# Top-16 picks of the second sequence moved into the task queue, value sums tied behind the gate masks, and both expert tables stored block by block

## The chip, the cores and the metric

The kernel runs on one core of one Trainium2 chip. The metric is the device time of one execution in microseconds. TensorE (PE) multiplies matrices and has its own weight loads (PEld); VectorE (DVE), ScalarE (ACT) and GpSimd (POOL) do the rest. SyncE (SP) and POOL issue nearly all transfers, which share 16 DMA engines. All engines take their instructions in the order in which the program lists them, so an instruction that waits holds up everything listed behind it on that engine.

## The reference

Two sequences of 256 tokens (prompt and sample), model width 1024, go through the same layer: short gated convolution and attention side by side, an output projection, and then the part that fills most of the time, a PEER mixer with 16,384 experts:

```python
q = (xf @ wq).reshape(T, PEER_HEADS, 2, PEER_HALF)            # 8 heads, two halves
s = jnp.einsum('thpc,hpnc->thpn', q, subkeys)                 # 128 keys per half
sv, si = lax.top_k(s, PEER_TOPK)                              # 16 of 128
cand = sv[..., 0, :, None] + sv[..., 1, None, :]              # 256 pairs
cv, cp = lax.top_k(cand, PEER_TOPK)                           # 16 of them
gates = softmax(cv)
a = gelu(einsum('thkd,td->thk', u_tab[eidx], x)) * gates      # 128 experts per token
out = einsum('thk,thkd->td', a, v_tab[eidx])
```

Each expert has a row of 1024 floats in `u_tab` and one in `v_tab`, 64 MiB a table.

## The kernel before

**Two ways through the mixer.** The prompt's 256 tokens take the direct way: for each of 2 tiles of 128 tokens and each of the 128 picks, POOL gathers one row of u and v beside each other per token (`grow`, 128 x 2048 floats, 1 MiB, L178), 256 gathers in all. For each, DVE takes the dot product with x (L208, `grow<-grow,xh`), ACT makes gelu and gate of it (L197, `dots`), and DVE adds the weighted v row to the output (L188, `xh<-grow,dots,xh`, called the value sum below). Four buffers (a ring) hold gathered rows. The sample's 256 tokens take the dense way: all experts are computed on PE. 128 blocks of u, each 128 experts (`ub`, 512 KiB, L995), are multiplied with the normalised input (`pSj`, stage "experts"); a dense gate matrix is built beside this from one-hot masks (`oi`, `oj` on DVE, scaled to `gh`, `gl` on ACT, multiplied to `pgm` on PE, L919 and L920); gelu times gate lands in `Al` and `Ah`. Then 128 blocks of v are multiplied with these and summed in four PSUM banks (`acc`, L1046, stage "values", two blocks of 512 KiB a transfer, L1026). Every third value block is split into two parts of lower precision and takes three products.

**Order of the stages.** `front` (norm, convolution, attention, projection) of the prompt, its query projections and picks of tile 0, `front` of the sample beside the prompt's first gathers and the picks of tile 1, the sample's query projections (L885, `pqq`), experts, values.

**What sets the order around the change.** The prompt's gathers are interleaved with everything else by a credit rule. Each step of PE work calls `bg(us)` (L254): it adds `us * share["b"]` to a credit from which tasks (generators that yield their cost) are run, and `us * share["a"]` to a credit from which one `gather()` is made per 2.65 (`GU`); without tasks both shares go to gathers up to `SMAX`. A gather also waits for the PE instruction that was last listed when it was issued (`sync_dep`, L148). What is left of the 256 when the values begin (`left`, L1018) is spread evenly over the value blocks (L1049). The frame's scheduler then sorts the instructions of each engine; a manual dependency (`order`, L183) stops it from listing one ahead of another. In the kernel before, the sample's picks are not a task: `step1` (L860) lists them at once when a head's scores are there, with gathers mixed in by `SR`. Three half heads' scores stay behind (`lag=3`), and come after the first expert blocks (`rest`, L1002). `gates_dense` (L894) is the one task of the experts.

**Start.** `weights` (L112) loads a weight slice and at once lists its split into `whi` (ACT) and `wlo` (DVE); for the first slice that is before the norm of the first input tile (L494).

Of the kernel before, what the change touches and what calls it, by code (L numbers as in the profile page):

```python
# [8 lines left out]
F32 = mybir.dt.float32  # L9
# [3 lines left out]
AF = mybir.ActivationFunctionType  # L13
# [7 lines left out]
NC = 8  # L21
# [15 lines left out]
JH = 92  # L37
SR = 0.6
SS = 0.72
SMAX = 0.74  # L40
SPL = 3
SBS = 0.42


@with_exitstack
def encoder_layer(ctx: ExitStack, tc: tile.TileContext, xp, xs_, meta, vec, w_in, w_out, wq,
# [22 lines left out]
    dve = Recorded(nc.vector, last)  # L69
    act = Recorded(nc.scalar, last_act)  # L70

    def sb(name, bufs, side="left"):
        return tc.tile_pool(name=name, bufs=bufs, side=side, reuse_waits="tile")

    def ps(name, bufs):
        return tc.tile_pool(name=name, bufs=bufs, space=PSUM, reuse_waits="tile")
# [34 lines left out]

    def weights(src, s, split=False):  # L112

        w = [wtile("w").rearrange("p (c n) -> p c n", c=4) for _ in range(2)]
        for q in range(2):
            nc.sync.dma_start(w[q], src[:, s, 4 * q:4 * q + 4])
        if not split:
            return lambda c, k=0: w[c // 4][:, c % 4]
        k = 1 + 2 * spl[0]
        spl[0] = 1 - spl[0]  # L120
        hl = [ga[k + i].tile([P, 2 * D], F32R, tag="g", name=n).rearrange("p (q x) -> p q x", q=2)
              for i, n in enumerate(("whi", "wlo"))]
        for q in range(2):
            f = w[q].rearrange("p c n -> p (c n)")
            act.activation(hl[0][:, q], f, AF.Copy)
            dve.tensor_tensor(hl[1][:, q], f, hl[0][:, q].bitcast(F32), op=ALU.subtract)
        v = [x.rearrange("p q (c n) -> p (q c) n", c=4) for x in hl]
        return lambda c, k=0: v[k][:, c]

# [52 lines left out]

    def order(i, before):  # L183
        tc.add_manual_dep(i.ins, before.ins.name,
                          mybir.DependencyInfo(mybir.DependencyClass.NoSync, mybir.DependencyReason.DATA),
                          reason="order")

    def g_val():  # L188
        t, k, r = vals.pop(0)
        before = last[0]  # L190
        i = dve.scalar_tensor_tensor(gctx["h"], r[:, D:], dots[:, k:k + 1], gctx["h"], op0=ALU.mult, op1=ALU.add)
        order(i, before)
        if t == 0 and k == P - 1:
            pool.dma_start(yp[0:P, :], gctx["h"])
            gctx["h"] = gctx["next"][1]
# [18 lines left out]

    direct = [False]

    def gather(n=1):
# [43 lines left out]
    def more(us):  # L261
        credit["a"] += us
        while credit["a"] >= GU:
            credit["a"] -= GU
            gather()
# [109 lines left out]
    def projections(xr, sk, scores, qp, step=None, split=False, rescale=None, lag=1):  # L375

        rn = None
        late = []

        def key_scores(hp, qs, pl=None, tag="tr"):  # L380
            pn = (pl or pst).tile([P, 2, P], F32, tag=tag, name="pn")
            for t in range(2):
                pe.matmul(pn[:, t, :], qs[:, t * P:(t + 1) * P], sk[:, hp, :], start=True, stop=True)
            if hp < 2 and rn is not None:
                for t in range(2):
                    act.activation(scores[:, hp, t], pn[:, t], AF.Copy, scale=rn[:, t:t + 1])
            else:
                act.activation(scores[:, hp], pn, AF.Copy)
            if step is not None and hp % 2:
                step(hp // 2)  # L390

        for hd in range(PH):
            w = weights(wq, hd, split)
            for pp in range(2):
                pq = psm.tile([P, 256], F32, tag="mm", name="pqq")
                mm(pq, lambda c, k: w(c, k)[:, pp * P:(pp + 1) * P], xr, split=split)
                qs = qp.tile([P, 256], F32, tag="qs", name="qs", bufs=lag + 1)
                act.activation(qs, pq, AF.Copy)
                late.append((2 * hd + pp, qs))
                if len(late) > lag:  # L400
                    key_scores(*late.pop(0))
                if hd == 0 and rescale is not None:
                    rn = rescale(xr, pp)
                bg(3.9)
        if lag > 1:
            return lambda pl, tag: late and key_scores(*late.pop(0), pl, tag)
        key_scores(*late.pop(0))
# [20 lines left out]
    nc.sync.dma_start(vecs, vec)  # L428
    w_kv = weights(w_in, 0, True)
    nc.sync.dma_start(hs_[:, 1, :], xp[P:2 * P, :])  # L430
# [38 lines left out]
    def front(s, h, rn):  # L469
# [17 lines left out]
        for t in range(2):  # L487
# [5 lines left out]
            if sp:  # L493
                dve.tensor_scalar_mul(x, h[:, t, :], stat)  # L494
            else:
                act.activation(x, h[:, t, :], AF.Copy, scale=stat)
# [363 lines left out]
    def step1(hd):  # L860
        share["a"] = 0.0
        for us in heads1(hd, [0, 1]):
            more(us * SR)
        topk_left[0] -= 1

    rows = []

    def rescale(xr, pp):

        if pp == 0:  # L870
            on = q1.tile([P, P], F32, name="on", bufs=1)
# [11 lines left out]

    share.update(a=SR, b=0.0)
    rest = projections(xr1, sk1, sc1, q1, step1, rescale=rescale, lag=3)  # L885
    direct[0] = True
    pfs.close()
    psS = ctx.enter_context(ps("psS", 2))
    psgx = ExitStack()
    psg = psgx.enter_context(ps("psg", 2))  # L890
    r_done = [0]
    tau = [0]

    def gates_dense():  # L894
# [4 lines left out]
        topk_left[0] = -1  # L899
        yield 6.0  # L900
        ogx = ExitStack()
# [34 lines left out]
        for t in range(2):  # L936
# [14 lines left out]
            yield 1.6  # L951
            yield 3.0
            for o in range(P // OC):
                s0 = o * OC
# [5 lines left out]
                ib = iv[:, None, :, :].to_broadcast([P, OC, 64, 2])  # L960
                dve.tensor_tensor(v4(oi), sl4(0), ib, op=ALU.is_equal)
                dve.tensor_tensor(v4(oj), sl4(1), ib, op=ALU.is_equal)
# [4 lines left out]
                if len(steps) > 1:  # L967
                    gate_products(*steps.pop(0))
                if o == 0:
                    yield 2.0  # L970
                yield 1.3 + (4 * r_done[0] + 60) / 700
        gate_products(*steps.pop(0))
# [17 lines left out]
    for j in range(P):  # L990
# [3 lines left out]
        ub = wtile("u")  # L994
        nc.sync.dma_start(ub, u_t[:, j])  # L995
        if j % SG == 0:
# [6 lines left out]
        if j == 3:  # L1003
            tasks.append(gates_dense())
            share.update(a=SS, b=SBS)
        bg(3.5)
# [8 lines left out]
    acc = [[pacc.tile([P, 512], F32, name=f"acc{t}_{q}") for q in range(2)] for t in range(2)]  # L1015
    vn3 = v_n.rearrange("(i j) d -> i j d", j=P)
    vhl = gc.tile([P, 2, D], F32R, tag="xr", name="vhl")
# [4 lines left out]
    def values(j):  # L1022

        if j % 2 == 0:
            vpair[0] = vp.tile([P, 2, D], F32, tag="v", name="v")
            nc.sync.dma_start(vpair[0], vn3[:, j:j + 2])  # L1026
        vb = vpair[0][:, j % 2]
# [37 lines left out]
def layout(**inputs):  # L1065
# [15 lines left out]
    def wl(a):  # L1081
# [27 lines left out]
        qkg=qkg, gffn=g("norm_ffn_g"), rope=rope, iota16=iota, dec=dec,  # L1109
        u_t=c(u.reshape(P, P, NC, P).transpose(3, 1, 2, 0).reshape(P, P, D)), uv=c(np.concatenate([u, v], axis=1)), v_n=v)  # L1110

# [18 lines left out]
```

## Time and profile before

| | us |
|---|---|
| median of 3 runs | 1346.87 (1346.04 to 1347.17) |
| the profiled execution's own time | 1346.99 |
| its span, first to last instruction | 1345.2 |
| sample's query projections begin (first `pqq`) | 334.2 |
| experts begin (first `pSj`) | 408.6 |
| values begin (first `acc`) | 926.3 |
| last `acc` ends | 1341.1 |

1.8 us of the profiled execution lie outside its span. PE is busy in 95% of the span, DVE in 78%, and the DMA engines move 342 GB/s on average, over 410 GB/s in most slices of the second half. So no single engine is idle enough to be ruled out, and the question for each stage is which of PE and the transfers ends last. A busy PE is not one at its best: a matmul that runs at half clock counts as busy too, which is why the granted clock is read beside it.

### The profile page before, as it was taken

The numbers are of one execution on the slowest core, as the hardware profiler recorded it, in microseconds if no ns is written. First come the engines' busy times: TensorE is split into PE (matmuls) and PEld (weight loads), VectorE is DVE, ScalarE is ACT, GpSimd is POOL, SyncE is SP. The second block draws the span as 40 slices with busy tenths as digits, with TensorE's granted clock in tenths as the row PEclk, the third lists the DMA queues.
The fourth block names the chain that finished last, engine by engine and source line by source line (L and its number), as shares of the span: only waits on it lengthen the run. The fifth ranks groups of instructions, "written<-read, shape, count | busy, mean of one in ns | idle before, by whom it ended". The sixth has DMA issues, their size and how long they took to land.

```text
span 1345.2 us, 17868 instructions
## 1 busy us (share of the span) xinstructions
PE 1275.6 (95%) x6038; PEld 965.0 (72%) x6038; DVE 1056.0 (78%) x2279; ACT 549.9 (41%) x1621; POOL 389.1 (29%) x480
## 2 busy tenths in 40 slices
PE   6999998998898999969999999996999999999998
PEld 5888996777787887758888888884555555555554
DVE  5656998885799998679888787897677777777767
ACT  5555641742221311148776555663222222222221
POOL 1111223431223343543233232231222232222221
PEclk9999998998999999989999999997999999999999
DMA  5534636658998999999999999997999999999997
GB/s 174 160 108 152 214 106 219 216 192 317 365 333 309 383 417 415 416 412 386 399 396 399 397 415 354 409 403 275 410 420 422 421 420 415 420 420 418 415 422 324
DMA packets 80859, 459.68 MB, mean 342 GB/s; under 512 B 9456, under 2 KB 9968, under 8 KB 39552
## 3 DMA queue, kind: packets, MB, share of 16 engines
q0 software_dynamic: 37296, 270.02, 50.1%
q1 hardware_dynamic: 42032, 183.57, 35.9%
q10 hardware_dynamic: 1440, 4.95, 1.0%
q8 instruction: 47, 0.77, 0.2%
q14 instruction: 44, 0.36, 0.1%
HBM read 454.28 MB, written 4.19 MB: 341 GB/s over the span
## 4 chain that ended last, share of the span: by engine, by line
PE 37%; DMA 17%; DVE 7%; issue 3%; ACT 2%; POOL 0%; DVEq 0%; POOLq 0%; ACTq 0%; SPq 0%
PE acc L1046 27%; DMA grow<-in_uv,eidx 16%; PE pSj L136 9%; DVE xh L63 3%; DVE grow L63 2%; DMA v<-in_v_n 1%; DVE Ah L63 1%; ACT dots L63 1%; DVE Al L63 1%; PE pgm L920 1%; PE pgm L919 1%; ACT gh L63 0%; ACT pSj L63 0%; DVE vhl L63 0%; ACT gl L63 0%
## 5 line engine op out<-in xcount | busy, mean ns | idle before, releaser
L178 POOL DMA_INDIRECT grow<-in_uv,eidx x256 | 317.2, 1239 | 717.2 <-DVE xh L63 233.5
L136 PE MATMUL pSj<-xr,u 128*128 128x256 f32 x2048 | 468.9, 386 | 7.4 <-ACT Ah L63 4.7
L136 PEld LDWEIGHTS pSj<-xr,u 128*128 128x128 f32 x2048 | 386.2, 192 | 69.0 <-DMA u<-in_u_t 7.5
L63 DVE SCALAR_TENSOR_TENSOR xh<-grow,dots,xh 128x1024 f32<-128x1024 f32 x256 | 328.2, 1282 | 58.4 <-ACT dots L63 57.2
L63 DVE SCALAR_TENSOR_TENSOR grow<-grow,xh 128x1024 f32<-128x1024 f32 x256 | 312.5, 1221 | 70.2 <-DMA grow<-in_uv,eidx 69.2
L63 ACT ACTIVATE dots<-dots 128x1 f32<-128x1 f32 x256 | 51.7, 202 | 544.8 <-DVE grow L63 544.4
L1046 PE MATMUL acc<-v,Al 128*128 128x512 f32 x496 | 220.1, 597 | 5.1 <-DMA v<-in_v_n 5.1
L1046 PEld LDWEIGHTS acc<-v,Al 128*128 128x128 f32 x496 | 94.9, 191 | 113.0 <-issue 110.5
L1046 PE MATMUL acc<-vhl,ah 128*128 128x512 f32 x336 | 107.4, 441 | 0.0
L63 ACT ACTIVATE gh<-oj,ghi 128x128 f16<-128x128 f16 x256 | 99.5, 389 | 6.2 <-PE pgm L919 5.7
L63 ACT ACTIVATE gl<-oj,glo 128x128 f16<-128x128 f16 x256 | 99.5, 389 | 0.0
L63 DVE TENSOR_TENSOR vhl<-v,vhl 128x1024 fp32r<-128x1024 f32 x42 | 51.4, 1224 | 55.6 <-ACT vhl L63 55.6
L1046 PEld LDWEIGHTS acc<-vhl,ah 128*128 128x128 f32 x336 | 63.2, 188 | 30.2 <-issue 19.1
L1046 PE MATMUL acc<-v,Ah 128*128 128x512 f32 x192 | 84.3, 592 | 0.0
L63 ACT ACTIVATE dots<-dots,gate_all 128x1 f32<-128x1 f32 x256 | 74.6, 292 | 7.0
L63 DVE TENSOR_TENSOR wlo<-w,whi 128x1024 fp32r<-128x1024 f32 x42 | 51.1, 1218 | 19.6 <-ACT whi L63 13.4
L1046 PEld LDWEIGHTS acc<-v,Ah 128*128 128x128 f32 x192 | 36.4, 190 | 41.2 <-issue 40.2
L136 PE MATMUL pqq<-xr,w 128*128 128x256 f32 x256 | 60.0, 388 | 0.8 <-DMA w<-in_wq 0.8
L136 PEld LDWEIGHTS pqq<-xr,w 128*128 128x128 f32 x256 | 48.6, 195 | 8.1 <-DMA w<-in_wq 1.4
L919 PE MATMUL pgm<-gh,oi 128*128 128x128 f16 x256 | 36.8, 222 | 16.1 <-DVE oi L63 15.1
L63 ACT ACTIVATE vhl<-v 128x1024 fp32r<-128x1024 f32 x42 | 44.0, 1048 | 19.1 <-DMA v<-in_v_n 18.4
L63 ACT ACTIVATE whi<-w 128x1024 fp32r<-128x1024 f32 x42 | 43.9, 1058 | 18.3 <-PE pqq L136 8.5
(279 smaller groups left out, 1753.6 us busy)
## 6 DMA issues: line engine op xcount, KB each, us to landing
u<-in_u_t SPq DMA_DIRECT2D x128, 512.0 KB, 8.6
v<-in_v_n SPq DMA_DIRECT2D x64, 1024.0 KB, 8.9
w<-in_w_in SPq DMA_DIRECT2D x36, 512.0 KB, 3.9
w<-in_wq SPq DMA_DIRECT2D x32, 512.0 KB, 6.1
w<-in_w_out SPq DMA_DIRECT2D x16, 512.0 KB, 4.7
grow<-in_uv,eidx POOLq DMA_INDIRECT x256, 10.1
hdram<-h ACTq DMA_DIRECT2D x3, 512.0 KB, 2.7
h<-in_xp SPq DMA_DIRECT2D x2, 512.0 KB, 5.9
```

The source lines that it names most:

```text
L63: i = f(*a, **k)
L136: i = pe.matmul(out, st_(c, a), mv(c, b), start=(n == 0), stop=(n == NC * len(terms) - 1))
L178: i = pool.indirect_dma_start(out=r, out_offset=None, in_=uv, in_offset=bass.IndirectOffsetOnAxis(ap=eidx[:, t, k:k + 1], axis=0))
L919: pe.matmul(pg[:, q, :], oi[:, r, :], gh[:, r, :], start=True, stop=False)
L920: pe.matmul(pg[:, q, :], oi[:, r, :], gl[:, r, :], start=False, stop=True)
L1046: i = pe.matmul(acc[t][q], a[:, t * P:(t + 1) * P], v[:, q * 512:(q + 1) * 512], start=j == 0 and n == 0, stop=j == P - 1 and n == len(ter ...
```

## The change

There are five edits.

1. The sample's picks become tasks. `step1` only appends `heads1(...)` to the task list; the shares during the projections are a = 0.57 and b = 0.58 (was 0.6 and 0.0, with the picks listed at once), and they stay until the gate masks begin, where a = 0.75 and b = 0.46 (was 0.72 and 0.42 from block 3 on). `SMAX` is 0.66 (was 0.74). The gate task's yields are a little smaller.
2. A value sum may not be listed ahead of the newest `oi` mask on DVE.
3. `u_t` and `v_n` are stored so that one block is one contiguous run of memory; the load of block j is `u_t[j]`, of a value pair `v_n[j // 2]`. Bytes and shapes of the transfers are the same.
4. The split of the first weight slice is listed behind the norm of the first input tile.
5. The PSUM buffers of `pSj` are laid behind those of the gate products; and the row scale `rescale` of the sample comes two half heads later (4 scores instead of 2 are scaled on ACT).

```diff
-SR = 0.6
-SS = 0.72
-SMAX = 0.74
+SR = 0.57
+SRB = 0.58
+SSG = 0.75
+SMAX = 0.66
-SBS = 0.42
+SBS = 0.46
...
-    def weights(src, s, split=False):
+    def weights(src, s, split=False, late=False):
...
+        def convert(behind=None):
+            for q in range(2):
+                f = w[q].rearrange("p c n -> p (c n)")
+                act.activation(hl[0][:, q], f, AF.Copy)
+                i = dve.tensor_tensor(hl[1][:, q], f, hl[0][:, q].bitcast(F32), op=ALU.subtract)
+                if behind is not None:
+                    order(i, behind)
...
         order(i, before)
+        if last_oi[0] is not None:
+            order(i, last_oi[0])
...
-            if hp < 2 and rn is not None:
+            if hp < 4 and rn is not None:
...
-                if hd == 0 and rescale is not None:
-                    rn = rescale(xr, pp)
+                if hd < 2 and pp and rescale is not None:
+                    rn = rescale(xr, hd)
...
-                dve.tensor_scalar_mul(x, h[:, t, :], stat)
+                i = dve.tensor_scalar_mul(x, h[:, t, :], stat)
+                if t == 0:
+                    convert_kv(i)
...
     def step1(hd):
-        share["a"] = 0.0
-        for us in heads1(hd, [0, 1]):
-            more(us * SR)
-        topk_left[0] -= 1
+        tasks.append(heads1(hd, [0, 1]))
...
-    share.update(a=SR, b=0.0)
+    share.update(a=SR, b=SRB)
...
-    psS = ctx.enter_context(ps("psS", 2))
     psgx = ExitStack()
     psg = psgx.enter_context(ps("psg", 2))
+    psS = psgx.enter_context(ps("psS", 2))
...
-        yield 6.0
+        yield 3.0
...
+            share.update(a=SSG, b=SBS)
             for o in range(P // OC):
...
-                dve.tensor_tensor(v4(oi), sl4(0), ib, op=ALU.is_equal)
+                last_oi[0] = dve.tensor_tensor(v4(oi), sl4(0), ib, op=ALU.is_equal)
...
-                if o == 0:
-                    yield 2.0
-                yield 1.3 + (4 * r_done[0] + 60) / 700
+                yield 1.2 + (4 * r_done[0] + 60) / 760
...
-        nc.sync.dma_start(ub, u_t[:, j])
+        nc.sync.dma_start(ub, u_t[j])
...
-            share.update(a=SS, b=SBS)
...
-            nc.sync.dma_start(vpair[0], vn3[:, j:j + 2])
+            nc.sync.dma_start(vpair[0], v_n[j // 2])
...
-        u_t=c(u.reshape(P, P, NC, P).transpose(3, 1, 2, 0).reshape(P, P, D)), ..., v_n=v)
+        u_t=c(u.reshape(P, P, NC, P).transpose(1, 3, 2, 0).reshape(P, P, D)), ..., v_n=c(v.reshape(P, P // 2, 2, D).transpose(1, 0, 2, 3)))
```

The order shows three places. First, DVE at the start of the program, before (`ss` is the sum of squares, `xs` the normalised tile):

```order
L63 TENSOR_SCALAR ss_169<-ss_169 128x1
L63 TENSOR_TENSOR wlo<-w,whi 128x1024
L63 COPY sel<-ident 2x128
L63 TENSOR_TENSOR wlo<-w,whi 128x1024
L63 TENSOR_SCALAR xs<-h_123,stat 128x1024
```

And the same place after:

```order
L64 TENSOR_SCALAR ss_165<-ss_165 128x1
L64 COPY sel<-ident 2x128
L64 TENSOR_SCALAR xs<-h_123,stat 128x1024
L64 TENSOR_TENSOR wlo<-w,whi 128x1024 x2
L64 SCALAR_TENSOR_TENSOR lo<-pt,vecs,xT 128x128
```

Both `wlo` moved behind `xs`. Second, PE where the query projections (`pqq`, key scores `pn`) give way to the experts (`pSj`), before:

```order
L136 MATMUL pqq<-xr,w 128x256 x8
L383 MATMUL pn<-Ah,qs 128x128 x5
L136 MATMUL pSj<-xr,u 128x256 x16
L383 MATMUL pn<-Ah,qs 128x128
L136 MATMUL pSj<-xr,u 128x256 x8
L383 MATMUL pn<-Ah,qs 128x128 x2
L136 MATMUL pSj<-xr,u 128x256 x304
L938 LDWEIGHTS idx_i
```

And after, where the last row is again the first transpose of the gate stage:

```order
L149 MATMUL pqq<-xr,w 128x256 x8
L394 MATMUL pn<-Ah,qs 128x128 x2
L149 MATMUL pSj<-xr,u 128x256 x8
L394 MATMUL pn<-Ah,qs 128x128 x2
L149 MATMUL pSj<-xr,u 128x256 x8
L394 MATMUL pn<-Ah,qs 128x128 x2
L149 MATMUL pSj<-xr,u 128x256 x8
L394 MATMUL pn<-Ah,qs 128x128 x2
L149 MATMUL pSj<-xr,u 128x256 x376
L948 LDWEIGHTS idx_i
```

The late scores now stand one by one behind an expert block, and the gate stage begins after 400 `pSj` (50 blocks) instead of 328 (41 blocks). Third, DVE where the first masks are made, before:

```order
L63 TENSOR_TENSOR oj<-dup,io 128x512
L63 SCALAR_TENSOR_TENSOR xh<-grow,dots,xh 128x1024
L63 SCALAR_TENSOR_TENSOR grow,dots<-grow,xh 128x1024
L63 SCALAR_TENSOR_TENSOR xh<-grow,dots,xh 128x1024
L63 SCALAR_TENSOR_TENSOR grow,dots<-grow,xh 128x1024
L63 SCALAR_TENSOR_TENSOR xh<-grow,dots,xh 128x1024
L63 SCALAR_TENSOR_TENSOR grow,dots<-grow,xh 128x1024
L63 SCALAR_TENSOR_TENSOR xh<-grow,dots,xh 128x1024
L63 TENSOR_TENSOR oi<-dup,io 128x512
L63 SCALAR_TENSOR_TENSOR grow,dots<-grow,xh 128x1024
```

And after:

```order
L64 TENSOR_TENSOR oi<-dup,io 128x512
L64 TENSOR_TENSOR oj<-dup,io 128x512
L64 SCALAR_TENSOR_TENSOR xh<-grow,dots,xh 128x1024
L64 SCALAR_TENSOR_TENSOR grow,dots<-grow,xh 128x1024
L64 TENSOR_TENSOR oi<-dup,io 128x512
L64 TENSOR_TENSOR oj<-dup,io 128x512
L64 SCALAR_TENSOR_TENSOR xh<-grow,dots,xh 128x1024
L64 SCALAR_TENSOR_TENSOR grow,dots<-grow,xh 128x1024
L64 TENSOR_TENSOR oj<-dup,io 128x512 x2
L64 TENSOR_TENSOR oi<-dup,io 128x512
```

Before, four value sums and three dot products stood between the third `oj` group and the next `oi`; after, there is one pair between masks.

## Rows read from the trace of the kernel before

**Rows 1.** Busy time by stage: projections, experts (two parts), values; (x) counts instructions.

```profile
core 0: us, PE busy (x) PEld busy (x) DVE busy (x) ACT busy (x) POOL busy (x), PEclk, DMA share, GB/s
334.20:408.60 74.40, 65.38 (x322) 56.79 (x320) 63.28 (x263) 18.35 (x67) 20.82 (x44) 0.98 0.94 343
408.60:582.00 173.40, 171.22 (x761) 142.69 (x762) 150.28 (x365) 38.49 (x111) 72.09 (x71) 0.99 0.99 393
582.00:926.30 344.30, 321.07 (x1813) 277.26 (x1811) 286.29 (x445) 223.89 (x774) 106.09 (x87) 0.96 0.99 392
926.30:1341.10 414.80, 414.14 (x1192) 225.81 (x1192) 306.10 (x384) 103.55 (x281) 112.07 (x96) 0.99 0.98 406
```

**Rows 2.** PE's waits: for whom, us in total, times, longest us.

```profile
PE pgm L919 <- DVE oi L63: 15.1, 2, 9.6
...
PE acc L1046 <- DMA v<-in_v_n: 5.1, 1, 5.1
PE pSj L136 <- ACT Ah L63: 4.7, 1, 4.7
PE pb L877 <- ACT dg L63: 3.5, 1, 3.5
```

**Rows 3.** Busy time in three stretches at half clock (columns of Rows 1).

```profile
343.60:347.00 3.40, 3.40 (x10) 2.69 (x9) 2.44 (x7) 0.00 (x0) 1.00 (x1) 0.50 0.87 303
...
596.20:609.80 13.60, 7.03 (x22) 5.66 (x23) 11.40 (x18) 8.78 (x32) 5.75 (x5) 0.50 0.99 372
917.00:930.70 13.70, 5.47 (x14) 2.66 (x15) 5.81 (x10) 3.13 (x9) 1.18 (x1) 0.50 0.94 370
```

**Rows 4.** Expert blocks' own instructions in three stretches: PE, PEld, DVE, ACT, clock, DMA.

```profile
424.80:466.20 41.40, 41.40 (x194) 36.44 (x193) 0.00 (x0) 3.03 (x3) 1.00 0.96 365
510.50:555.90 45.40, 44.54 (x193) 35.54 (x193) 0.00 (x0) 3.01 (x3) 1.00 1.02 416
...
852.80:898.80 46.00, 43.45 (x193) 35.81 (x193) 3.09 (x3) 3.47 (x6) 1.00 1.02 409
```

**Rows 5.** Gate products' own instructions in the last of these: PE, DVE, ACT.

```profile
852.80:898.80 46.00, 5.52 (x75) 4.65 (x8) 1.11 (x5) 1.00 1.02 409
```

**Rows 6.** Value products' own instructions: PE, PEld, DVE, clock, DMA share, GB/s.

```profile
1005.50:1044.00 38.50, 38.50 (x114) 21.19 (x113) 0.00 (x0) 1.00 1.02 422
```

**Rows 7.** Instructions on gathered rows by stage: DVE, POOL (one per gather issued).

```profile
0.00:334.20 334.20, 41.94 (x52) 21.04 (x19) 0.98 0.54 185
334.20:408.60 74.40, 32.52 (x41) 13.85 (x14) 0.98 0.94 343
...
926.30:1345.20 418.90, 243.65 (x298) 112.07 (x96) 0.99 0.98 404
```

**Rows 8.** Timeline of the start: DVE and ACT; start, duration, [idle before <-releaser].

```profile
9.28 1.23 DVE L63 TENSOR_TENSOR wlo<-w,whi 128x1024 fp32r<-128x1024 f32 x1 [3.51 <-ACT whi L63]
...
10.94 1.06 ACT L63 ACTIVATE sq<-h 128x1024 f32<-128x1024 f32 x1 [0.27 <-DMA h<-in_xp]
...
11.85 0.75 DVE L63 TENSOR_SCALAR xs<-h,stat 128x1024 f32<-128x1024 f32 x1
...
13.80 0.37 ACT L63 ACTIVATE xT<-pt,vecs 128x128 fp32r<-128x128 f32 x1 [0.54 <-PE pt L461]
```

**Rows 9.** Timeline where the gate products begin: DVE and PE.

```profile
601.55 0.42 DVE L63 TENSOR_TENSOR oi<-dup,io 128x512 f16<-128x512 f16 x1
...
602.03 0.29 PE L919 MATMUL pgm<-gh,oi 128*128 128x128 f16 x1 [9.58 <-DVE oi L63]
```

**Rows 10.** SP's first value loads, and a stretch in which they alone run.

```profile
921.27 33.90 SPq L1026 DMA_DIRECT2D v<-in_v_n  x7
...
925.00:929.00 4.00, 2.74 (x4) 1.22 (x5) 0.00 (x0) 0.37 (x1) 0.00 (x0) 0.50 1.01 426
```

**Rows 11.** DVE groups during the projections: count, busy us, mean ns, idle before.

```profile
L63 DVE SCALAR_TENSOR_TENSOR xh<-grow,dots,xh 128x1024 f32<-128x1024 f32 x15 | 19.2, 1281 | 1.6 <-ACT dots L63 1.5
L63 DVE SCALAR_TENSOR_TENSOR grow<-grow,xh 128x1024 f32<-128x1024 f32 x13 | 15.7, 1209 | 8.1 <-DMA grow<-in_uv,eidx 8.1
```

More of the change, by code (lines that the diff above doesn't have):

```diff
@@ L70, in encoder_layer, with order @@
     act = Recorded(nc.scalar, last_act)
+    def order(i, before):
+        tc.add_manual_dep(i.ins, before.ins.name,
+                          mybir.DependencyInfo(mybir.DependencyClass.NoSync, mybir.DependencyReason.DATA),
+                          reason="order")
     def sb(name, bufs, side="left"):
@@ L122, in weights @@
               for i, n in enumerate(("whi", "wlo"))]
[L123 to L126, printed above, removed]
+        def convert(behind=None):
[5 more added lines that the diff above has]
+                    order(i, behind)
         v = [x.rearrange("p q (c n) -> p (q c) n", c=4) for x in hl]
+        if late:
+            return convert, lambda c, k=0: v[k][:, c]
+        convert()
         return lambda c, k=0: v[k][:, c]
@@ L181, in g_issue @@
         pend.append((t, k, r))
[L183 to L186, printed above, removed]
     def g_val():
@@ L215, in encoder_layer @@
     direct = [False]
+    last_oi = [None]
     def gather(n=1):
@@ L428, in encoder_layer @@
     nc.sync.dma_start(vecs, vec)
-    w_kv = weights(w_in, 0, True)
+    convert_kv, w_kv = weights(w_in, 0, True, True)
     nc.sync.dma_start(hs_[:, 1, :], xp[P:2 * P, :])
@@ L860, in step1, with rescale @@
     def step1(hd):
-        share["a"] = 0.0
-        for us in heads1(hd, [0, 1]):
-            more(us * SR)
-        topk_left[0] -= 1
+        tasks.append(heads1(hd, [0, 1]))
     rows = []
-    def rescale(xr, pp):
-        if pp == 0:
+    def rescale(xr, hd):
+        if hd == 0:
             on = q1.tile([P, P], F32, name="on", bufs=1)
@@ L1015, in encoder_layer @@
     acc = [[pacc.tile([P, 512], F32, name=f"acc{t}_{q}") for q in range(2)] for t in range(2)]
-    vn3 = v_n.rearrange("(i j) d -> i j d", j=P)
     vhl = gc.tile([P, 2, D], F32R, tag="xr", name="vhl")
@@ L1109, in layout @@
         qkg=qkg, gffn=g("norm_ffn_g"), rope=rope, iota16=iota, dec=dec,
-        u_t=c(u.reshape(P, P, NC, P).transpose(3, 1, 2, 0).reshape(P, P, D)), uv=c(np.concatenate([u, v], axis=1)), v_n=v)
+        u_t=c(u.reshape(P, P, NC, P).transpose(1, 3, 2, 0).reshape(P, P, D)), uv=c(np.concatenate([u, v], axis=1)), v_n=c(v.reshape(P, P // 2, 2, D).transpose(1, 0, 2, 3)))
 def kernel(**inputs):
```

## The prediction

> **What bounds the kernel now.** I read the profile in this order: busy time by stage, PE's waits, the clock, then the pace of the blocks in each stage. By stage [rows 1] PE is busy nearly all the time and the DMA engines too: from 408.6 us on both stand at 93% or more. So a stage can be bound by either, and the pace of the blocks tells which. Twelve expert blocks took 41.4 us where the transfers moved 365 GB/s, and 45.4 us where they moved 416 GB/s [rows 4]. The first is PE's own pace (3.45 us a block, no gate products in between); in the second, PE was slowed by the transfers. Twelve value blocks took 38.5 us at 422 GB/s [rows 6]; PE was busy throughout and waited for values only at the stage's start [rows 2], so I read that as PE's pace too (3.21 us a block), with the transfers just below their limit. PE's waits are few but long [rows 2], and three of them are followed by half clock [rows 3]: 1.2 instead of 2.4 GHz for 3.4, 13.6 and 13.7 us.
>
> I count transfers in units of 1 MiB (1.0486 MB): a gather is one, a value pair one, an expert block a half. At 416 GB/s a unit takes 2.52 us, at 422 GB/s 2.485 us. Four expert blocks with four gathers are 6 units, 15.1 us, which is what rows 4 show (45.4 / 3); with three gathers they are 5 units, 12.6 us, less than PE's 13.8.
>
> **The change part by part.** The sum goes by the profiled execution, 1346.99 us, of which 1345.2 us are span; it lies 0.1 us above the median of the runs shown.
>
> *Start.* The first tile's `xs` stood behind two `wlo` of 1.23 us until 11.85 us, and ACT's first `xT` began at 13.80 us [rows 8]. Afterwards `xs` needs neither, and `xT` follows ACT's second Square, which ends at 12.00 us. That gives 1.8 us; the `wlo` then lie beside PE's transposes. Bounds: 0 (the split's second half is needed next) and 4.4 us (back to the first `wlo`'s start at 9.28 us). I take 1.8, the nearer row.
>
> *Projections (74.4 us).* PE waited 3.5 us for the row scale (`pb` for `dg`) and 4.7 us for `Ah` before the first expert block [rows 2]. `pb` now stands 5 matmuls later (16 instead of 11 `pqq` behind the last transposes), 5 x 3.45 / 8 = 2.2 us; a wait of 1.3 us stays, and I let the half clock behind it go, worth half of 3.4 us. The 4.7 us go because `pSj` no longer takes the PSUM banks that the late scores must leave. Gain 2.2 + 1.7 + 4.7 = 8.6 us; at worst 0, when ACT stands behind a late dot product as before. The picks are now spread over the first 35 or so expert blocks. That they fit: DVE was busy 63.28 + 150.28 = 213.6 us from 334.2 to 582.0 [rows 1]. The order has 5 dot products fewer ahead of the first mask (48, was 53), 5 x (1281 + 1209) ns = 12.5 us [rows 11], so 201 us of work. PE needs 74.4 - 8.6 = 65.8 us, and 50 x 3.45 us more, 238 us to where the gate stage begins now. DVE has 37 us to spare.
>
> *Experts (517.7 us).* PE's own time is 128 x 3.45 = 441.6 us and 512 gate products at (46.0 - 41.4) / 75 = 0.061 us [rows 4, 5], 31.4 us, so 473 us. 44.7 us are lost. I can name 32: (a) blocks 20 to 43 at the transfers' pace, 24 x (45.4 - 41.4) / 12 = 8.0 us. (b) The first gate products: PE waited 9.6 us for an `oi` that stood on DVE behind value sums and dot products, which in turn waited for gathers [rows 2, 9], and then ran at half clock; 7.03 us of busy time there [rows 3] is 3.5 us lost. Together 13.1 us. (c) The end: 5.5 us for the last `oi` (15.1 - 9.6) and 5.1 us for the first value block, which SP could only issue at 921.27 us, behind the last gate products [rows 2, 10], and I put 0.7 us to half clock there, 11.3 us in all. Afterwards (a) goes: the credit rule gives 0.57 x 3.5 / 2.65 = 0.75 gathers a block (was 0.72 x 3.5 / 2.65 = 0.95). From the masks on it gives 0.99, but then PE has 13.8 + 32 x 0.061 = 15.8 us for four blocks against 15.1 us of transfers. Of (b) I leave 4 us: the tie puts the masks ahead of the value sums and the transfers are no longer behind, but only 3 blocks lie between the transposes and the first product, before it was 6. (c) goes: the last gate product now stands behind block 123, so nothing is left at the end and the first value pair is loaded beside the last blocks. Gain 8.0 + 9.1 + 11.3 = 28.4 us; bounds 0 (all three waits come back elsewhere) and 44.7.
>
> *Values (414.8 us).* Here the bill comes. Counting gathers through the credit rule, 99 are left for the value stage before and 110 after. The trace agrees with the 99: 96 were issued in that stage [rows 7], 3 before it. So 107 are to be issued, with 63 value pairs and 1 more unit: 171 x 2.485 = 424.9 us, and I add 3 us because the first gather waits for block 1. Before it was 161 x 2.485 = 400 us, below PE's 128 x 38.5 / 12 = 410.7 us. The stage turns from PE's to the transfers': 428 us, 13.2 us more. The half clock that cost 2.2 us at its start [rows 3] goes and is covered by that. Bounds for a unit: 2.46 us (426 GB/s, in a stretch in which value loads ran alone [rows 10]) and 2.52 us, so 421 and 434 us.
>
> *Layout.* I cost it at nothing. Value loads alone, with their old row distance of 512 KiB, moved 426 GB/s [rows 10], and the mix in the experts 416 GB/s [rows 4]: no row shows strided blocks to be slow. Bounds: 0, and what takes the value stage back to PE's pace (below). The Trainium skill, "DMA: Bandwidth & Descriptors", section "Latency and other measured facts", has copies with a row pitch of 512 KiB at 207 GB/s, and full rate when tiles are contiguous. [...]
>
> Sum: 1346.99 - 1.8 - 8.6 - 28.4 + 13.2 = 1321.4 us.
>
> **Rivals.** *Gathers slip (slower).* If the dot products and value sums, now tied behind masks that wait for PE, fall behind in the experts, gathers are issued late, since a ring buffer comes free only with its value sum. Each one that slips into the value stage costs 2.485 us there. For: at 408.6 us only 19 + 14 = 33 had been issued [rows 7] where the rule had listed 37, and ACT will be tight: 223.89 us of it [rows 1] for 64 mask steps is 3.5 us a step, against 3.94 us of PE per block and step. Against: DVE has 37 us to spare until the masks. From 10 late gathers on the gain is gone (25.6 / 2.485); with 12 late ones it is 1321.4 + 29.8 = 1351 us.
>
> *Waits in the mask stretch (less gain).* 31 blocks in a row now carry a mask step each. One event like the one at 602 us, 13.1 us, gives 1334 us. For: the ACT load. Against: with 25 products per four blocks PE lost nothing [rows 4, 5].
>
> *The gain is given back whole (no change).* The wait at the first gate products and those in the projections stay as they are, 9.1 + 8.6 us, and the values take 434 us, 6 us more: 1345 us. For: both hang on DVE's queue. Against: the transfers, for which that queue waited, have room now.
>
> *Layout counts (more gain).* If the contiguous blocks shorten every value load and leave gathers more room, the value stage falls back to PE's 410.7 us: 1304 us. Rows 10 speak against it; this is also the direction of the page's rule.
>
> **How the numbers follow.** Forecast 0.62, slipping gathers 0.14, waits in the mask stretch 0.12, given back whole 0.07, layout 0.05. A difference of 0.2% is what a measurement of this kernel can tell from none: 1344.2 to 1349.6 us. Faster is forecast, mask stretch and layout, 0.79; same 0.07; slower 0.14. The forecast's own range is 1310 (unit of 2.46 us, no wait left at the gates, 2.6 us more at the start) to 1336 us (unit of 2.52 us, 8.6 us of the projections not gained). The range that I give reaches from 1307 to 1345 us; outside are the slower case and most of the layout's.
>
> **What would show it.** Start: first `xT` near 12 us. Projections: first `pSj` 66 us or so behind the first `pqq`, with no wait for `Ah`. Experts: 13.8 us for four blocks up to block 48, no half clock of 13 us near the first `pgm`, none at the change to the values, first value load issued ahead of the last expert block; about 489 us in all. Values: longer than 414.8 us, about 428, with 107 gathers issued there, PE waiting for value loads or for ACT behind a dot product, and 420 GB/s or more. The forecast is wrong if the values stay near 411 us (then the transfers had more room than I think), if more than about 112 gathers are issued there, or if new waits stand between blocks 52 and 84.

## The result, and the profile after

The changed kernel takes 1359.16 us (1357.05 to 1361.19, four runs) against 1346.70 us before: ratio 1.0093 [1.0075, 1.0110]. It is slower by 0.9%, where 1321.4 us was forecast. The profiled execution took 1361.19 us, 1359.4 us of it span. (One of the twelve executions of e6 below took 4591 us; the median and the ratio shown there are those of the other eleven.)

By stage (projections, experts up to block 51, experts from block 52, values; columns of [rows 1]):

```profile
334.10:410.00 75.90, 66.90 (x316) 58.28 (x315) 52.49 (x184) 18.59 (x66) 23.24 (x37) 0.93 0.90 336
410.00:606.30 196.30, 187.28 (x849) 161.69 (x848) 157.98 (x439) 42.25 (x118) 64.33 (x76) 0.97 0.93 358
606.30:910.90 304.60, 297.55 (x1733) 259.05 (x1732) 260.65 (x412) 215.44 (x744) 90.53 (x78) 0.99 1.00 393
910.90:1354.40 443.50, 423.29 (x1193) 224.28 (x1191) 335.86 (x421) 108.92 (x306) 125.89 (x108) 0.99 1.00 411
```

The front ends where it ended before (334.1 us, 334.2). The projections take 75.9 us (forecast 65.8, before 74.4), the experts 196.3 + 304.6 = 500.9 (forecast 489.3, before 517.7), the values 443.5 (forecast 428, before 414.8). So 16.8 us were won in the experts and 28.7 us paid in the values. The columns on the right tell why: up to block 51 the DMA engines are busy 0.93 of the time and move 358 GB/s; before they were at 0.99 and 393 in nearly the same stretch [rows 1]. What was not moved there is moved in the values, where they are full (1.00). Gathers issued in the same four stretches (POOL's instructions that write `grow`):

```profile
334.10:410.00 75.90, 16.49 (x14) 0.93 0.90 336
410.00:606.30 196.30, 50.62 (x41) 0.97 0.93 358
606.30:910.90 304.60, 88.81 (x75) 0.99 1.00 393
910.90:1354.40 443.50, 125.89 (x108) 0.99 1.00 411
```

108 in the values stand against 96 before [rows 7]. PE's waits behind the front (for whom, us in total, times, longest):

```profile
PE acc L1053 <- DVE al L64: 18.3, 14, 2.7
PE pSj L149 <- ACT Al L64: 8.6, 2, 6.7
PE pgm L929 <- DVE oi L64: 6.3, 1, 6.3
PE pqq L149 <- DVE xr L64: 5.7, 1, 5.7
PE pt L750 <- DVE h L64: 3.3, 1, 3.3
```

The four waits of [rows 2] are gone or shorter, and others have come: for `xr` in the projections, for `Al` among the picks, for `oi` at the change from the first mask tile to the second (863.7 us), and fourteen for `al` in the values. With three of them goes half clock, as in [rows 3]:

```profile
359.60:366.40 6.80, 5.70 (x13) 4.55 (x14) 6.80 (x14) 0.45 (x3) 1.28 (x2) 0.50 0.93 348
489.30:496.10 6.80, 4.96 (x12) 3.98 (x13) 6.73 (x17) 2.66 (x6) 1.01 (x1) 0.50 0.78 320
861.40:868.20 6.80, 4.52 (x17) 3.82 (x18) 6.80 (x13) 5.16 (x20) 2.37 (x2) 0.50 0.93 338
```

The value products' own instructions in a stretch of 12 blocks, which took 38.5 us before [rows 6]:

```profile
1199.90:1243.40 43.50, 39.35 (x114) 20.94 (x113) 0.00 (x0) 1.00 1.01 418
```

At full clock and with the same 114 products PE now needs 43.5 us, with the DMA engines full: the transfers set the pace. The stage's full part and its end (columns of [rows 1]):

```profile
920.00:1340.00 420.00, 400.06 (x1130) 212.74 (x1129) 318.64 (x400) 103.21 (x292) 123.52 (x106) 0.99 1.01 416
1340.00:1354.40 14.40, 14.13 (x38) 6.74 (x36) 12.28 (x17) 3.24 (x10) 1.19 (x1) 1.00 0.64 258
```

While the DMA engines are full they move 416 GB/s, 2.52 us a unit of 1 MiB; in the last 14.4 us, when little is left to move, 258 GB/s.

### The profile page after: what moved, and what is told of

Same layout as the page of the kernel before. It is cut to its first block, busy times and chain, and to the rows that moved or that the text cites. A ratio compares the mean times of both kernels' runs of the same rounds, so it can differ in the third digit from the quotient of the medians.

```text
span 1359.4 us, 17884 instructions
## 1 busy us (share of the span) xinstructions
PE 1280.3 (94%) x6038; PEld 967.5 (71%) x6038; DVE 1054.7 (78%) x2276; ACT 550.6 (41%) x1622; POOL 384.9 (28%) x480
## 4 chain that ended last, share of the span: by engine, by line
PE 21%; DMA 18%; DVE 17%; issue 7%; ACT 5%; POOL 0%; DVEq 0%; POOLq 0%; ACTq 0%
DMA grow<-in_uv,eidx 18%; PE pSj L149 14%; DVE xh L64 7%; PE acc L1053 6%; DVE grow L64 4%; DVE Al L64 2%; ACT dots L64 2%; DVE vhl L64 2%; ACT vhl L64 1%; DMA v<-in_v_n 1%; ACT gh L64 1%; DVE al L64 0%; DVE Ah L64 0%; ACT Al L64 0%; ACT Ah L64 0%
## 5 line engine op out<-in xcount | busy, mean ns | idle before, releaser
L191 POOL DMA_INDIRECT grow<-in_uv,eidx x256 | 304.5, 1189 | 722.9 <-DVE xh L64 206.7
L1053 PE MATMUL acc<-vhl,al 128*128 128x512 f32 x168 | 49.0, 414 | 18.7 <-DVE al L64 18.3
L1053 PEld LDWEIGHTS acc<-vhl,al 128*128 128x128 f32 x168 | 29.8, 189 | 34.4 <-DVE al L64 29.2
L64 ACT ACTIVATE whi<-w 128x1024 fp32r<-128x1024 f32 x42 | 43.5, 1058 | 15.9 <-PE pqq L149 8.5
```

Source lines behind the costliest of these rows:

```text
L64: i = f(*a, **k)
L191: i = pool.indirect_dma_start(out=r, out_offset=None, in_=uv, in_offset=bass.IndirectOffsetOnAxis(ap=eidx[:, t, k:k + 1], axis=0))
L1053: i = pe.matmul(acc[t][q], a[:, t * P:(t + 1) * P], v[:, q * 512:(q + 1) * 512], start=j == 0 and n == 0, stop=j == P - 1 and n == len(ter ...
```

## The experiments

Theory A: the change is slow because its lower share of gathers in the projections and the first 50 expert blocks leaves 11 more for the values. Theory B: it is slow because of what it moved on DVE, ACT and POOL (picks, tie, masks). Each ratio is against the kernel before, run beside it, with its 95% interval; that kernel's own median there was 1343.9 to 1346.7 us, so rows are compared by their ratios; "left" counts the gathers that, in the order, still lack their dot product at the change to the values.

| kernel | left | values, us | median, us | ratio |
|---|---|---|---|---|
| before / changed | 99 / 110 | 414.8 / 443.5 | 1346.7 / 1359.2 | 1 / 1.0093 [1.0075, 1.0110] |
| e1 before, lower share | 110 | 446.1 | 1374.0 | 1.0225 [1.0199, 1.0250] |
| e2 changed, 11 left out | 99 | 413.5 | 1330.3 | 0.9899 [0.9874, 0.9924] |
| e3 before, new layout | 99 | 414.9 | 1345.1 | 0.9989 [0.9965, 1.0013] |
| e4b before, gate stage | 98 | 419.2 | 1338.8 | 0.9962 [0.9941, 0.9982] |
| e6 changed, share mended | 99 | 415.3 | 1338.9 | 0.9954 [0.9924, 0.9984] |
| e7 before, front parts | 99 | 415.3 | 1347.9 | 1.0022 [0.9993, 1.0051] |
| e9 e4b and e7 together | 98 | 419.8 | 1343.2 | 0.9986 [0.9962, 1.0010] |
| e10 before, tie alone | 99 | 413.4 | 1344.1 | 0.9980 [0.9952, 1.0007] |
| e11 e6, `cd` on DVE | 99 | 422.2 | 1346.8 | 1.0018 [0.9998, 1.0037] |
| e12 e6 without e7's parts | 99 | 415.5 | 1340.6 | 0.9979 [0.9953, 1.0004] |
| e13 e6, share moved | 99 | 418.9 | 1352.1 | 1.0044 [1.0019, 1.0068] |
| e14 e4b with a lull | 98 | 420.0 | 1341.2 | 0.9973 [0.9955, 0.9991] |

**e1, the lower share alone, on the kernel before.**

```diff
-SS = 0.72
+SS = 0.65
```

> The kernel before with one number changed: SS 0.65 instead of 0.72, so that 110 gathers are left for the value stage, as in the changed kernel (before 99). Nothing else of the change. Theory A (it is the share of gathers left for the value stage that costs): the transfers are idle more in the experts and the value stage grows by 11 units of 2.5 us, 27 us at most, while the experts win at most the 8 us of blocks 20 to 43; values 435 to 442 us, whole 1360 to 1368 us. Theory B (the ties and the picks as tasks make the value stage long, by dot products that stand in new places on DVE): values stay at 415 to 425 us and the whole at 1340 to 1350 us.

Experts (two parts) and values:

```profile
408.80:583.00 174.20, 172.33 (x770) 144.33 (x771) 151.66 (x368) 43.89 (x126) 71.99 (x71) 0.98 0.97 389
583.00:916.50 333.50, 317.61 (x1804) 274.89 (x1802) 259.07 (x409) 214.64 (x736) 88.16 (x76) 0.98 0.96 369
916.50:1362.60 446.10, 426.56 (x1192) 226.38 (x1192) 333.15 (x417) 107.53 (x303) 126.94 (x107) 0.98 0.98 403
```

One number makes the value stage as long as the whole change does, 31 us more; the experts win 10.0 us (507.7). B falls as the cause of the loss. A had the direction, and its sizes were too small: 446.1 us against 435 to 442 for the values, 1374.0 us against 1360 to 1368 for the whole. PE's waits near the first gate products in the same run:

```profile
PE pgm L919 <- ACT gh L63: 3.4, 1, 3.4
PE pSj L136 <- ACT Al L63: 0.3, 1, 0.3
```

The wait of 9.6 us for `oi` [rows 2, 9] is gone, without any tie; 3.4 us for `gh` stand there instead.

**e2, the changed kernel with 11 gathers of the second prompt tile left out** (their dot products and value sums too).

```diff
+    del queue[-11:]
     left = len(queue) + len(pend)
```

> The changed kernel, but 11 of the second prompt tile's 128 gathers (with their dot products and value sums) are left out, so that 99 stand before the value stage as before the change. Theory A (the units of transfer left over set the value stage): 443.5 - 11 x 2.52 = 416 us for the values, whole 1331 to 1334 us. Theory B (the waits of PE for al behind dot products, 18 us, set it): they do not go with the count, values 430 us or more, whole 1346 us or more.

```profile
905.20:1318.70 413.50, 412.67 (x1193) 224.46 (x1191) 308.78 (x388) 104.41 (x284) 116.69 (x97) 1.00 1.00 414
```

As A says: PE is busy for 412.67 of 413.5 us, and the waits for `al` are down from 18.3 to 0.2 us, so they were an effect of the 11 gathers. That it was their transfers, and not the work on DVE that went with them, is a reading: the DMA engines were full in both runs, DVE was busy for about three quarters of the stage in both. The 11 gathers cost 443.5 - 413.5 = 30 us, 2.7 us each. The row also shows that with 99 left the stage is at both limits: PE is full, and the DMA engines are at 1.00.

**e6, the changed kernel with the share mended; nothing is left out.**

```diff
-SR = 0.57
+SR = 0.70
```

> The changed kernel with one number changed: SR 0.70 instead of 0.57, so that 99 gathers are left for the value stage instead of 110; nothing is left out. Theory A (the share of gathers is what made the change slow, the rest of it is a gain): values back to 411 to 416 us, experts 505 to 512 us (11 more gathers there at 2.5 us, partly in transfer time that stood idle), whole 1334 to 1342 us, faster than before. Theory B (the picks as tasks and their waits eat the gain as well; with more gathers early the dot products stand behind transfers again): experts 515 us or more, whole 1345 us or more.

```profile
409.60:615.50 205.90, 188.94 (x850) 161.88 (x848) 179.54 (x496) 41.77 (x118) 84.15 (x92) 0.98 0.96 381
615.50:923.20 307.70, 300.73 (x1731) 259.25 (x1732) 264.18 (x421) 218.43 (x759) 95.48 (x80) 0.99 1.00 395
923.20:1338.50 415.30, 413.03 (x1193) 224.59 (x1192) 311.09 (x390) 104.95 (x286) 112.66 (x97) 1.00 1.00 414
```

A holds in the values and in the sign: faster than before, and 1.4% below the changed kernel (ratios 0.9954 and 1.0093). The experts take 205.9 + 307.7 = 513.6 us, between what the two theories gave: up to block 51, where 50 gathers were issued instead of 41, they take 9.6 us more than in the changed kernel (205.9 against 196.3), and behind it, with two gathers more, 3.1 us. PE's waits among the picks (first row) and in all of the mask stretch:

```profile
PE pSj L149 <- ACT Al L64: 14.7, 4, 5.3
PE pgm L929 <- ACT gh L64: 1.4, 1, 1.4
PE pgm L929 <- DVE oi L64: 1.0, 1, 1.0
```

So with the gathers back, the waits for `Al` grew from 8.6 to 14.7 us, but the long wait for `oi` at the first gate products did not return.

**e3, the layout alone.**

```diff
-nc.sync.dma_start(ub, u_t[:, j])
+nc.sync.dma_start(ub, u_t[j])
-nc.sync.dma_start(vpair[0], vn3[:, j:j + 2])
+nc.sync.dma_start(vpair[0], v_n[j // 2])
```

> The kernel before with the new layout alone: each expert block and each value pair one contiguous run in memory. My step cost it at nothing: 1346 to 1348 us, transfers in the value stage at 422 GB/s as before. The rival that layout counts: the value stage and blocks 20 to 43 shorter, 1338 us or less; or, if contiguous runs meet in the same banks, slower, 1350 us or more.

```profile
928.10:1343.00 414.90, 414.13 (x1192) 225.67 (x1192) 305.98 (x384) 103.40 (x281) 110.53 (x96) 0.99 0.98 406
```

No difference in time, and the values move 406 GB/s with either layout [rows 1]. There PE sets the pace, though (414.13 of 414.9 us busy), so the test of the layout is a stretch of expert blocks in which the transfers set it (columns of [rows 4]):

```profile
485.00:563.00 78.00, 76.72 (x336) 62.01 (x335) 0.00 (x0) 5.02 (x5) 1.00 1.02 416
```

That is the 416 GB/s of the old layout in that part of the experts [rows 4].

**e10, the tie alone** (the line in `g_val`, and `last_oi` set at each first mask).

```diff
+        if last_oi[0] is not None:
+            order(i, last_oi[0])
```

> The kernel before with the tie alone (a value sum never stands ahead of the last listed mask). My step (b) gave the tie most of 9.1 us at the first gate products: the wait for oi at 602 us (9.6 us) at most 4 us, half clock of 13.6 us gone, whole 1337 to 1341 us. Theory B (that wait comes from dot products that wait for gathers, which the tie does not move, and went in the changed kernel since the transfers were idle there): the wait stays above 7 us, whole 1344 to 1349 us.

```profile
PE pgm L922 <- DVE oi L63: 9.6, 1, 9.6
PE pgm L923 <- ACT gl L63: 0.8, 1, 0.8
```

The wait is the old one to a tenth, and so is the half clock behind it (13.7 us long). The time is not told apart from before. With e1: the wait came from dot products that stood ahead of `oi` and waited for gathers; fewer gathers took most of it away, the tie did not.

**e4b, the gate stage alone**: tie as in e10, and masks that end earlier.

```diff
-SBS = 0.42
+SBS = 0.44
-        yield 6.0
+        yield 3.0
-                if o == 0:
-                    yield 2.0
-                yield 1.3 + (4 * r_done[0] + 60) / 700
+                yield 1.2 + (4 * r_done[0] + 60) / 760
```

> The kernel before with the gate stage of the change alone: the value sums tied behind the masks, the masks listed earlier (3.0 instead of 6.0, 1.2 + (4 r + 60) / 760, SBS 0.44), but the picks of the second prompt as before, the share of gathers as before (98 left), old layout. Theory A (the loss is the share of gathers, while the mask step was priced rightly): the end of the experts wins the 11.3 us of my step (c), the value stage stays at 412 to 418 us; whole 1333 to 1339 us. Theory B (earlier masks push gathers out just as the whole change did): gathers issued in the value stage above 104, values 430 us, whole 1345 us or more.

Blocks 40 to 47, the rest of the experts, and the values:

```profile
551.10:599.90 48.80, 39.44 (x192) 31.69 (x193) 41.47 (x67) 32.48 (x114) 19.99 (x14) 0.90 1.00 398
599.90:913.20 313.30, 308.00 (x1736) 267.11 (x1733) 259.78 (x398) 198.88 (x685) 97.06 (x80) 0.99 0.99 394
913.20:1332.40 419.20, 414.03 (x1192) 225.97 (x1192) 309.63 (x388) 104.47 (x284) 110.46 (x97) 1.00 0.99 410
```

Theory A's side: faster, with 97 gathers in the values. The experts take 507.9 us, 9.8 us less than before. Of my step (c) the wait for `oi` is gone and 1.4 us for the first value block are left, but PE then waited 4.6 us for `vhl`, the split of the third value block, so the values are longer. And blocks 40 to 47 cost 48.8 us, where 64 gate products and 8 blocks need 31.5 (8 x 3.45 + 64 x 0.061).

**e7, three small parts alone**: late first conversion, row scale later (its diff below), PSUM order.

```diff
-if hd == 0 and rescale is not None:
-    rn = rescale(xr, pp)
+if hd < 2 and pp and rescale is not None:
+    rn = rescale(xr, hd)
```

> The kernel before with three small parts of the change alone: the late first conversion, the row scale later, and the PSUM order; read stage by stage. My forecast for them: start 1.8, row scale 3.9, wait for Ah 4.7, 10.4 us together, projections about 66 us long. Theory B, after the trace of the changed kernel: the start gives nothing (even again by 22 us), the 4.7 us go and come back as a wait for Al in the first 12 blocks, the row scale comes back as a wait behind a dot product; projections 72 us or more and the sum within 4 us.

Projections 74.8 us and ratio 1.0022: B. PE's waits in the projections and first blocks:

```profile
PE pqq L148 <- DVE xr L63: 3.1, 1, 3.1
PE pt L746 <- DVE h L63: 2.9, 1, 2.9
PE pb L886 <- ACT dg L63: 2.0, 1, 2.0
PE pn L390 <- ACT Ah L63: 1.8, 1, 1.8
```

The waits removed [rows 2] stand one step further on. The wait for `h` is not one of them: e3, e4b and e10, which are as before up to there, have it too (3.4 to 4.5 us).

**e9, e4b and e7's parts together**; of these the PSUM order:

```diff
-    psS = ctx.enter_context(ps("psS", 2))
     psgx = ExitStack()
     psg = psgx.enter_context(ps("psg", 2))
+    psS = psgx.enter_context(ps("psS", 2))
```

> All parts of the change but the picks as tasks, the share of gathers (98 left) and the layout: late conversion, row scale, PSUM order, tie, masks that end earlier. If the parts add, 1338.8 (the gate stage alone) less what the front parts give: 1330 to 1336 us, faster than both kernels. If the waits only move: 1338 us or more. Against the changed kernel with its share mended it tells what the picks as tasks are worth.

The parts don't add: not told apart from before, and no gain on e4b. Nor can it be told from e6, so what the picks as tasks are worth stays open.

**e12, e6 with the first conversion, row scale, PSUM order and layout as before.** What is left of the change, beside tie, masks and shares, is the picks as tasks:

```diff
-        share["a"] = 0.0
-        for us in heads1(hd, [0, 1]):
-            more(us * SR)
-        topk_left[0] -= 1
+        tasks.append(heads1(hd, [0, 1]))
```

> The back of the change alone with the mended share: picks as tasks, tie, masks that end earlier, 99 gathers left; first conversion, row scale, PSUM order and layout as before. Against the changed kernel with the mended share (1340.3) it tells what the front parts are worth there. My forecast gave them 10.4 us: then this one is at 1347 to 1351 us. Theory B (they are worth nothing or less, as the run of them alone says): 1334 to 1341 us.

Theory B: ratio 0.9979 beside e6's 0.9954, with intervals that overlap. The front parts are worth nothing that can be told in either company.

**e11, the pair sums of the picks on DVE, in e6.**

```diff
-pool.tensor_tensor(cd[:, :, o:o + n], s0[:, :, a:a + 1].to_broadcast([P, n_t, n]), ...
+dve.tensor_tensor(cd[:, :, o:o + n], s0[:, :, a:a + 1].to_broadcast([P, n_t, n]), ...
```

> The changed kernel with SR 0.70 (99 gathers left), and the pair sums of the picks (cd) on DVE instead of POOL. Theory A (the picks make PE wait for Al because POOL's queue couples them with the gathers: POOL stands at cd until DVE has come to the picks, 24 us in blocks 0 to 51, with the next gathers behind it): the waits for Al there, 14.7 us with the mended share, fall below 6 us, DVE grows by 10 us of small adds; whole 1328 to 1335 us. Theory B (DVE's own queue is full there and ACT's Gelu of Al stands behind weights of dot products): the waits stay at 10 us or more, whole 1338 to 1345 us.

PE's waits in blocks 0 to 51:

```profile
PE pSj L149 <- ACT Al L64: 11.6, 4, 5.8
```

14.7 us in e6: B. POOL's queue is not what makes the picks hold PE up. The whole, 1346.8 us, lies above B's range as well; the values took 422.2 us, and why was not found.

**e13, e6 with the gathers moved to the gate stage.**

```diff
-SR = 0.70
+SR = 0.64
-SSG = 0.75
+SSG = 0.80
```

> The changed kernel with 99 gathers left as in the run of the mended share, but the 11 moved elsewhere: SR 0.64 (was 0.57, mended 0.70) in the projections and the picks' blocks, SSG 0.80 (was 0.75) in the gate stage. Theory A (in the gate stage PE's own pace of 15.8 us for four blocks still covers 6.24 units, 15.7 us, while each gather among the picks makes waits): blocks 52 on stay at 15.8 us for four, experts some 506 us, whole 1333 to 1338 us. Theory B (only the number left counts, not where they go): 1338 to 1343 us, with blocks 52 on at 16 us or more for four.

Worse than either theory gave. From block 52 to the values PE waited four times for `oi`:

```profile
PE pgm L929 <- DVE oi L64: 7.6, 4, 2.5
```

Blocks 96 to 119 took 109.0 us (98.9 for blocks 96 to 119 in e6). Where the gathers go counts too. That the masks stand behind dot products on DVE there fits the four waits; no run isolates it.

**e14, e4b with a lull in the gathers ahead of the masks.**

```diff
+            share["a"] = 0.75
+        if j == 32:
+            share["a"] = 0.45
```

> The kernel before with the gate stage of the change (tie, masks that end earlier), and a lull in the gathers ahead of the first masks: the share of gathers is 0.45 instead of 0.72 from block 32 to the first mask, some 4 gathers fewer there, and 0.75 behind it, so that 98 are left for the value stage as without the lull. Theory A (the wait for oi and the half clock at the first gate products come from dot products that wait for late gathers, so transfers that have room there take it away; this, not the tie, is what the changed kernel won at that place): blocks 40 to 47 take some 31 us instead of 48.8, whole 1322 to 1332 us, faster than every kernel so far that computes everything. Theory B (DVE and ACT are full with masks there, whatever the transfers): blocks 40 to 47 stay at 44 us or more, whole 1337 us or more.

Not decided: the sizes are theory B's, but the edit did not do what it was meant to. 36 gathers were issued up to block 39, as many as in e4b, and 12 instead of 14 in the next eight blocks:

```profile
411.50:557.70 146.20, 53.13 (x36) 0.99 0.97 384
557.70:602.50 44.80, 16.80 (x12) 0.89 0.99 393
```

I read this as gathers that had been listed before block 32 and were late, so that the lull came too late for the place it was meant for. Blocks 40 to 47 took 44.8 us (48.8 in e4b), and the whole gained nothing on e4b.

e4b and e6 both beat the kernel before (by 0.4% and 0.5%) and the changed kernel.

## Why the prediction was wrong

The miss is 1361.19 - 1321.4 = 39.8 us of the profiled execution: values 15.5, experts 11.6, projections 10.1, start 1.7, end 0.9.

*Values (+13.2 forecast, +28.7).* The mechanism was right and the count nearly so (108 gathers issued, 107 forecast): the stage turned from PE's to the transfers'. The failed step is the term 171 x 2.485. Its rate came from one stretch of 422 GB/s, in which PE set the pace [rows 6]; the changed kernel moved 416 GB/s where the transfers set it, 2.52 us a unit, and 258 in its last 14.4 us, so 411 GB/s and 2.55 us a unit over the whole stage. 443.5 us at that rate are 174 units. 3 units x 2.485 + 174 x 0.066 - 3 us (the allowance at the start) are the 15.5 us, roughly. From the same step came a slack of 10.7 us between PE and the transfers before. e2 shows none: the 11 units cost 30 us, all of their time. (The lower bound of 421 us leaves out the 3 us that 428 and 434 include.) With this term right the forecast would have been 1336.9 us, still faster; with this miss alone taken away the changed kernel would be at 1345.7 us, as before. So it takes this miss and the others together to make the kernel slower, and e1 and e6 show that the value stage's part hangs on one number, the share.

*Experts (-28.4 forecast, -16.8).* (c) came true: block 124 to the values took 13.9 us (27.5 before), and no half clock stood there. (b) came true at its place and for another reason: the first gate product at 609.8 us waited for nothing, but e10 shows that the tie alone does nothing there and e1 that fewer gathers do. In the changed kernel fewer gathers are not the whole of it: e6 has as many left as before, and PE waits 1.4 us there. What else took the wait away (the picks spread out, the gate stage nine blocks later, the masks listed earlier) was not isolated; the tie and the masks listed earlier, without the rest, leave a wait of 5.5 us for `oi` (e4b). Of the 16.8 us won, 12.7 were bought with the gathers that the values paid for (500.9 against e6's 513.6). What failed is "DVE has 37 us to spare", from which I had the picks fit. Busy time fitted; order did not. ACT's Gelu of `Al` stood behind weights of dot products and an Exp that waited for DVE, PE waited 8.6 us, and half clock followed. The longer of the two waits ended at 491.14 us; on ACT (`gate_all` is the Exp's; start, duration, [idle before <-releaser]):

```profile
484.16 0.20 ACT L64 ACTIVATE dots<-dots 128x1 f32<-128x1 f32 x1 [3.85 <-DVE grow L64]
...
488.45 0.31 ACT L64 ACTIVATE gate_all<-gate_all 128x128 f32<-128x128 f32 x1 [2.45 <-DVE gate_all L64]
488.77 1.28 ACT L64 ACT_TABLE_LOAD   x1
490.07 1.02 ACT L64 ACTIVATE Al<-pSj 128x1024 f32<-128x1024 f32 x1
```

1.28 us of the wait is the second of two table loads (ACT_TABLE_LOAD) around the Exp. e6, e11 and e12 have these waits too (11.6 to 16.3 us), wherever `cd` is computed. Which of DVE's instructions is to blame was not isolated. At the tile change PE waited 6.3 us for `oi`, and 4.52 us of its work then ran at half clock: 8.6 us, the rival of the mask stretch at two thirds of its price. These waits and their half clock come to some 20 us; my 489.3 us held 4 us of the kind, and the sum of the stage is not closed further.

*Projections (-8.6 forecast, +1.5).* The wait for `Ah` did go, and the failed step is the row scale: 2.2 + 1.7 us were to be won, and a longer wait came. I asked how long `pb` would wait and not what stands ahead of the multiplications behind it. On DVE (start, duration, [idle before <-releaser]):

```profile
357.89 1.23 DVE L64 SCALAR_TENSOR_TENSOR grow<-grow,xh 128x1024 f32<-128x1024 f32 x1 [6.70 <-DMA grow<-in_uv,eidx]
...
360.24 2.73 DVE L64 TENSOR_TENSOR xr<-pb,xr 128x256 f32<-128x256 f32 x8
```

Eight multiplications stood behind a dot product that waited 6.70 us for its gather; PE waited 5.7 us for them and then ran at half clock for 6.8 us. e7 has the wait too (3.1 us), without the picks. The +1.5 us itself means little: in profiles of e1, e3, e4b, e10 and e14, whose code is as before up to there, the projections took 76.2 to 78.8 us, so 74.4 us was a short case. None is near 65.8 us.

*Start (-1.8 forecast, 0).* The step came true and bought nothing. `xT` began at 11.86 us (13.80 before [rows 8]), behind ACT's second Square as I had said, but then PE stood 3.01 us for it, and the second tile was next:

```profile
12.26 0.58 PE L149 MATMUL pkv<-whi,xT 128*128 128x256 f32 x1 [3.01 <-ACT xT L64]
...
19.15 0.67 PE L521 MATMUL pm<-ident,mt 16*128 16x16 f32 x8
```

Before, that transpose of `mt` stood at the same place:

```profile
19.21 0.66 PE L508 MATMUL pm<-ident,mt 16*128 16x16 f32 x8
```

*Rivals.* Gathers did not slip: 41 + 75 were issued in the experts as listed. The layout is worth nothing that can be told (e3). The Trainium skill, "DMA: Bandwidth & Descriptors", section "Latency and other measured facts", which the prediction names for this rival, has 207 GB/s for copies with a row pitch of 512 KiB beside 214 GB/s that the same measurement calls full, so at this pitch a loss of some 3%. In e3 no loss of the old layout shows (416 GB/s with either). None of my rivals had the right reason for a slower kernel. The nearest was in the forecast itself, as a bound of 434 us for the values: its 2.52 us a unit is what the full part of the stage showed, but 3 units and the slow end were missing. Nor did a sign that I had named for a wrong forecast show: the values did not stay near 411 us, 108 gathers are not more than 112, and PE was busy throughout from block 52 to 84.

## What to carry to other kernels

Where PE and the transfers are both full in the last stage, a transfer left over from an earlier stage costs its whole time (here 2.6 to 2.8 us for each gather of 1 MiB), so look first at what an edit does to the transfers' idle time in the earlier stages, and price a unit by the mean rate of a full stage, not by its best stretch. A wait that goes while fewer transfers run may not have been repaired: give the transfers back before counting it. In e6 that left the wait at the first gate products away and made the waits for `Al` longer. And busy time that fits on an engine says nothing about order: for each instruction that is moved, read which dot product, load or mask is now ahead of it.

## What the runs showed that I had not expected

Kernels with the same code up to there reached the sample's first `pqq` at 324.3 us (e10), 329.1 (e4b), 332.7 (e14) and 335.1 us (e3), so 11 us between executions come from the front alone; parts worth a few us have to be read stage by stage. Expert blocks of 512 KiB, beside gathers, moved no faster from contiguous memory than in rows 512 KiB apart (416 GB/s both). The same 11 gathers cost 12.7 us in the experts (e6, nine of them among the picks) and 28.2 us in the values (443.5 less e6's 415.3).
